# One turn of six raw weight tiles in the MLPs of a two-layer decoder, in place of two rings of three

## The chip, the cores and the metric

The kernel runs on one core of a Trainium2 chip. The metric is the device time of one execution in microseconds (us), the median of several runs. The engines are PE (TensorE: matmuls and transposes; PEld is its loading of weights), DVE (VectorE), ACT (ScalarE), POOL (GpSimd) and SP (SyncE, which here only issues DMAs). Each engine works through its own instructions in order, and an instruction that waits for a semaphore holds up those behind it on its engine.

## The reference

The input is 256 tokens of width D = 2048 in float32, and there are two layers.

```python
h = rmsnorm(x, g);   x = x + dsa_attention(h) @ a_w_out        # layer 1: an indexer picks keys
h = rmsnorm(x, g);   x = x + relu(h @ w_up[0])**2 @ w_down[0]   # D_FF = 8192
k, v = rmsnorm(x, g_kv) @ w_kv                                  # shared keys and values
h = rmsnorm(x, g);   x = x + dilated_attention(h @ b_w_q, k, v) @ b_w_out   # layer 2
h = rmsnorm(x, g);   x = x + relu(h @ w_up[1])**2 @ w_down[1]
out = rmsnorm(x, final_norm)
```

All weights are float32 and are read from memory once.

## The kernel before

**Products.** PE multiplies rounded float32 values ("fp32r"). To keep the accuracy, every operand is split in a high part, a cast (ACT, L190), and a low part, the difference to the original (DVE, L191). A product is then three matmuls, high by high, low by high and high by low (`mm3`, L194 to L196; the same three in `gemm`, L382). A weight tile therefore costs one DMA of 1 MB into a raw tile of 128 x 2 x 1024 values, a cast and a split for each 1024 columns, and then matmuls. The raw tile is free again when its last split has read it. High parts have four buffers, low parts three; within the MLPs one and two more.

**Raw tiles.** Those of the plain products and of all ordinary matrices (attention, projections, down matrix) are `wraw`, a ring of three in the pool `wp`. The pool "mlp", which is open from the middle of each output projection to the end of the MLP, has a second ring of three, `wx`, handed out by `pair_raw` (L239). Its users are the pairs of up tiles, the activations in `add_forms` (`gx`, L302), and in the end the vectors of the final norm (`fg`, L889).

**MLP.** It runs over eight blocks e of 1024 hidden columns: `up(0)`, `up(1)`, `down(0)`, `up(2)`, `down(1)` and so on. `up(e)` computes its 256 x 1024 block by a scheme with seven products for each pair of row blocks (`seven`, for three pairs; each reads two raw tiles, called x0 y0, x1 y1, x2 y2 here, 1 MB each, and forms five or so differences and sums of weights in place on DVE, L724 to L731, before it splits them) and four plain products from two further raw tiles (p0, p1). That is 25 products, 174 matmuls, 25 splits, 12 of those differences, and eight sums on the way out (L740 to L758). `down(e)` is an ordinary product, eight raw tiles d0 to d7, 192 matmuls. Its results are added to the residual `h` by DMAs of POOL that accumulate (L642); only the last block adds on DVE. The squared ReLU and the transposes of an up block are spread between the matmuls of the next block.

**Start of an MLP.** `project` multiplies the attention's output in two halves of 1024 columns. The first part of the depth (`CUT_A` = 8 tiles of 16 in layer 1, `CUT_B` = 14 in layer 2) is done for both halves, then the rest for the first half (O0), then `add_forms` for the first half, the rest for the second half (O1), and `add_forms` for the second half. `add_forms` squares h for the norm (ACT, L324), transposes h (PE, L292), scales it (ACT, L300 and L306), forms four sums on DVE and splits all of it into operands of the up blocks. U0 is `up(0)`.

**Order.** The kernel is written in the Tile language. Its scheduler sorts the instructions of each engine by priority, as they become ready in its own model of time, and buffers that come free in another order lead it to another sequence. All loads of weights go through SP's queue in that sequence, and a load waits at the head of the queue until its raw tile is free.

Of the kernel before, what the change touches and what calls it, by code (L numbers as in the profile page):

```python
# [11 lines left out]
F32 = mybir.dt.float32  # L12
# [5 lines left out]
P = 128  # L18
SEQ = 256
NT = SEQ // P  # L20
D = 2048
KC = D // P
# [19 lines left out]
GW = 1024  # L42
# [9 lines left out]
X0 = 2  # L52
ARRIVE = 2

HI_BUFS, LO_BUFS = 4, 3
HI_MORE, LO_MORE, RAW_MORE = 1, 2, 3

Q_W = NH * HD
# [5 lines left out]
NSM = ID + IH  # L64
# [28 lines left out]
def yoco_kernel(ctx: ExitStack, tc: tile.TileContext, x, a_w_in, a_w_out, w_kv, b_w_q, b_w_out, w_up, w_down,  # L93
# [7 lines left out]
    wp = ctx.enter_context(tc.tile_pool(name="wp", bufs=3))  # L101
# [3 lines left out]
    pools = {}  # L105
# [20 lines left out]
    def b2(dt=F32):  # L126
        return wk.tile([P, 512], dt, name="b2" + ("r" if dt == F32R else ""), tag="b2", bufs=8)
# [7 lines left out]
    def side():  # L135
        return ps2.tile([P, HALF], F32, name="side")
# [51 lines left out]
    def split(hi, lo, src):  # L188

        nc.scalar.copy(hi, src)  # L190
        nc.vector.tensor_tensor(lo, src, hi.bitcast(F32), op=ALU.subtract)  # L191
# [6 lines left out]
    def mm_wide(acc, w_hi, w_lo, xk, first, last):  # L198

        def both():  # L200
            nc.tensor.matmul(acc, w_hi, xk.rearrange("p a t -> p (a t)"), start=first, stop=last)

        if not last:
            both()
        nc.tensor.matmul(acc[:, :SEQ], w_lo, xk[:, 0], start=False, stop=False)
        if last:
            both()
# [28 lines left out]
        lo = lo_of.tile([P, GW], F32R, name="wlo", bufs=LO_BUFS if lo_of is wp else LO_MORE)  # L236
        return hi, lo

    def pair_raw():  # L239
        return pools["mlp"].tile([P, 2, GW], F32, name="wx", bufs=RAW_MORE)  # L240

    def norm_transpose(c4, which):

# [40 lines left out]
    def add_forms(halves, half, which):  # L284
        n, plain, f = halves[half]

        def transposed(c, c2):
            pt = side().rearrange("p (c t) -> p c t", c=2)
            for j in range(2):
                cc = 2 * c2 + j  # L290
                for t in range(NT):
                    nc.tensor.transpose(pt[:, j, t * P:(t + 1) * P], h[t][c][:, cc * P:(cc + 1) * P], ident)  # L292
                g = which * KC + 4 * c + cc
                yield cc, pt[:, j, :], gT[:, g:g + 1]

        if plain is not None:
            for c in range(2):
                for cc, pt, g in transposed(2 * half + c, 1):
                    hi, lo = plain[:, 2 * c + cc - 2, 0, :], plain[:, 2 * c + cc - 2, 1, :]
                    nc.scalar.activation(hi, pt, AF.Copy, scale=g)  # L300
                    nc.vector.scalar_tensor_tensor(lo, pt, g, hi.bitcast(F32), op0=ALU.mult, op1=ALU.subtract)
        gx = pair_raw()[:, :, :n * SEQ].rearrange("p c (j t) -> p c j t", t=SEQ)  # L302
        for c in range(2):
            for c2 in range(n // 2):
                for cc, pt, g in transposed(2 * half + c, c2):
                    nc.scalar.activation(gx[:, c, cc], pt, AF.Copy, scale=g)  # L306
        a11, a21, a12, a22 = gx[:, 0, :, :P], gx[:, 0, :, P:], gx[:, 1, :, :P], gx[:, 1, :, P:]
        s1, s2, s3, s4 = (b2()[:, :n * P].rearrange("p (q t) -> p q t", t=P) for _ in range(4))
        nc.vector.tensor_tensor(s1, a21, a22, op=ALU.add)
        nc.vector.tensor_tensor(s2, a11, s1, op=ALU.subtract)  # L310
        nc.vector.tensor_tensor(s3, a11, a21, op=ALU.subtract)
        nc.vector.tensor_tensor(s4, a12, s2, op=ALU.add)
        for name, v in (("a11", a11), ("a12", a12), ("s4", s4), ("s1", s1), ("s3", s3), ("s2", s2), ("a22", a22)):
            split(f[name][:, :, 0], f[name][:, :, 1], v)
# [37 lines left out]
    def load_w(w, r0, nk, cols, width):  # L352

        n = len(cols) * width
        raw = wp.tile([P, 2, GW], F32, name="wraw", bufs=3).rearrange("p a b -> p (a b)")[:, :nk * n]
        raw = raw.rearrange("p (k c) -> p k c", k=nk)
        joined = all(c == cols[0] + i * width for i, c in enumerate(cols))
        for i, c in enumerate(cols[:1] if joined else cols):
            m = n if joined else width
            nc.sync.dma_start(raw[:, :, i * width:i * width + m],  # L360
                              w[r0:r0 + nk * P, c:c + m].rearrange("(k p) c -> p k c", p=P))
        return raw
# [69 lines left out]
    take_x(0, raw_x, 0, X0)  # L432
    stat = stat_of(xa)
    cols_qi = (COL_QI, COL_QI + HALF)
    raw_w = wp.tile([P, 2, GW], F32, name="wraw", bufs=3)
    for c in range(2):
        nc.sync.dma_start(raw_w[:, 0, c * HALF:(c + 1) * HALF], a_w_in[0, :P, cols_qi[c]:cols_qi[c] + HALF])
    take_x(0, raw_x, X0, 4)
# [21 lines left out]

    def index_keys():

        raw = wp.tile([P, 2, GW], F32, name="wraw", bufs=3).rearrange("p a b -> p (a b)")[:, :KC * NSM]
        nc.sync.dma_start(raw.rearrange("p (k n) -> p k n", n=NSM),
                          a_w_in[0, :, COL_KI:COL_KI + NSM].rearrange("(k p) c -> p k c", p=P))
        acc = ps.tile([P, HALF], F32, name="acc")[:NSM]
        per = KC // 2
        for k0 in range(0, KC, per):
            hi, lo = (b[:, :per * NSM] for b in hi_lo())
            split(hi, lo, raw[:, k0 * NSM:(k0 + per) * NSM])  # L470
            for k in range(k0, k0 + per):
                xk = xa[k // 4][:, k % 4]
                r = slice((k - k0) * NSM, (k - k0 + 1) * NSM)
                mm_wide(acc, hi[:, r], lo[:, r], xk, k == 0, k == KC - 1)
        both = sum_halves(acc)
        pt = side()
        for t in range(NT):
            nc.tensor.transpose(pt[:, t * P:t * P + NSM], both[:, t * P:(t + 1) * P], ident[:NSM, :NSM])
        rstd = st.inv()
        rk = wk.tile([P, NT], F32, name="rk", tag="rk", bufs=2)  # L480
        nc.vector.tensor_scalar(rk, rstd, -SCALE, None, op0=ALU.mult)
        rA.extend((rstd, rk))
        kps = side()
        for t in range(NT):
            r = rstd[:, t:t + 1]
            kk = wk.tile([P, P + 176], F32, name="kk", bufs=1)[:, :P]
            src = pt[:, t * P:t * P + NSM]
            nc.scalar.activation(kk[:, :ID], src[:, :ID], AF.Copy, scale=r)
            nc.vector.tensor_scalar(wi[t], src[:, ID:], r, r, op0=ALU.mult, op1=ALU.mult)
            nc.vector.tensor_scalar(wi[t], wi[t], WI_SCALE, None, op0=ALU.mult)  # L490
            rope(kk[:, :ID].unsqueeze(1), 1, RI // 2, t, True)
            nc.vector.tensor_copy(kk[:, ID:], kk[:, :ID])
            nc.tensor.transpose(kps[:, t * P:(t + 1) * P], kk, ident)
        split(kiT[:, 0], kiT[:, 1], kps[:, :SEQ])
# [176 lines left out]
    def mlp(i, xm, st_in, gains_next, final=None):  # L671
# [4 lines left out]
        def up(e):  # L676
# [8 lines left out]
            c0 = e * GW  # L685
            cl, cr = slice(0, HALF), slice(HALF, GW)

            def raws(k1, tile_of):
                out = []
                for k in (k1, k1 + 4):  # L690
                    r = tile_of()
                    nc.sync.dma_start(r, w_up[i][k * P:(k + 2) * P, c0:c0 + GW].rearrange("(k p) c -> p k c", p=P))
                    out.append(r)
                return out
# [13 lines left out]
            rows = []  # L708

            def plain_rows():  # L710
                rows[:] = raws(2, lambda: wp.tile([P, 2, GW], F32, name="wraw", bufs=3))

            def plain(r, c):
                f = xm[0][2]
# [3 lines left out]
            def seven(half, pair, within=lambda: None, before_last=lambda: None):  # L718

                f = {name: v[:, pair:pair + 2] for name, v in xm[half][2].items() if name[0] != "p"}  # L720
                rx, ry = raws(8 * half + pair, pair_raw)
                b11, b12, b21, b22 = rx[:, :, cl], rx[:, :, cr], ry[:, :, cl], ry[:, :, cr]
                product(b11, (f["a11"], "q1"))
                nc.vector.tensor_tensor(b11, b12, b11, op=sub)  # L724
                product(b21, (f["a12"], "q2"))
                nc.vector.tensor_tensor(b12, b22, b12, op=sub)  # L726
                product(b22, (f["s4"], "q3"))
                nc.vector.tensor_tensor(b22, b11, b22, op=sub)  # L728
                product(b11, (f["s1"], "q5"))
                within()  # L730
                nc.vector.tensor_tensor(b21, b21, b22, op=add)  # L731
                product(b12, (f["s3"], "q7"))
                product(b22, (f["s2"], "q6"))
                before_last()
                product(b21, (f["a22"], "q4"))
# [150 lines left out]
    def final(ustat, w, row0, r2):  # L886


        both = pair_raw().rearrange("p a c -> p (a c)")  # L889
        fg = [both[:, s * HALF:(s + 1) * HALF] for s in range(4)]  # L890
        for s in range(4):
            nc.scalar.dma_start(fg[s], final_norm[s * HALF:(s + 1) * HALF].partition_broadcast(P))
# [35 lines left out]
        nk = GW // P  # L928
# [7 lines left out]
        for k in range(nk):  # L936
            if k % 2 == 0:
                raw = load_w(w, row0 + k * P, 2, (GW, GW + HALF), HALF)
            if k < 6:
                both = new_xt().rearrange("p c a t -> p (c a t)")  # L940
# [18 lines left out]
        for i in range(2):  # L959
            c = slice(i * HALF // 2, (i + 1) * HALF // 2)  # L960
# [41 lines left out]
```

## Time and profile before

| what | value |
|---|---|
| median of 3 runs | 2279.19 us (2277.17 to 2284.68) |
| the profiled execution, its own time | 2276.99 us |
| its span, first to last instruction | 2275.1 us |
| busy: PE, DVE, ACT | 2192.8, 1696.2, 1288.1 us |
| mean granted clock of PE | 0.984 |
| moved by DMA | 434.42 MB, mean 191 GB/s |

The span is what the rows of the profile add up to; the time of a run is about 2 us longer. "Busy" counts instructions under way. PE's matmuls overlap, so a matmul listed with 0.39 us starts 0.227 us after the one ahead of it. In the rows, `a <- b` after a line names what an engine waited for. The weight tile of an up block is `wx` (pairs) or `wraw` (plain), that of all else `wraw`.

### The profile page before, as it was taken

What the parts mean: (1) busy time and instruction counts of PE and PEld (TensorE: products, weight loads), DVE (VectorE), ACT (ScalarE), POOL (GpSimd) and SP (SyncE); (2) the same over time, 40 slices, a digit from 0 to 9 for tenths busy, and PEclk for the clock granted to TensorE, in tenths of its full rate; (3) what the DMA queues carried; (4) which work ended last, traced back from release to release, by engine and by line L of the source; (5) the groups of instructions that cost most, each with busy time, mean ns of one, the idle gap of its engine ahead of it and who ended that gap; (6) DMA issues with size and microseconds to landing.
All of it is one profiled execution on the core that took longest, in us unless ns stands there. A gap on an engine that the chain in (4) does not pass through costs nothing.

```text
span 2275.1 us, 27759 instructions
## 1 busy us (share of the span) xinstructions
PE 2192.8 (96%) x10310; PEld 1798.1 (79%) x10310; DVE 1696.2 (75%) x2267; ACT 1288.1 (57%) x1736; POOL 99.7 (4%) x118
## 2 busy tenths in 40 slices
PE   9999998999999999999999999998999999999998
PEld 7788866778788787788888888876777787787787
DVE  5877769777877867857577777669867867778675
ACT  6545556556656655556455555466556656565564
POOL 0000000011010010010000000000010010010100
PEclk9999999999999999999999999998999999999999
DMA  8554445667767566575554555554677576676754
GB/s 296 166 179 142 160 167 167 204 186 227 227 201 232 181 207 221 149 234 194 171 162 154 161 158 169 171 179 152 219 199 226 179 209 219 187 220 227 202 185 148
DMA packets 164103, 434.42 MB, mean 191 GB/s; under 512 B 12800, under 2 KB 62080, under 8 KB 163968
## 3 DMA queue, kind: packets, MB, share of 16 engines
q1 hardware_dynamic: 146688, 401.25, 52.7%
q0 software_dynamic: 16128, 29.37, 7.3%
q10 hardware_dynamic: 1152, 2.04, 0.3%
q8 instruction: 81, 1.33, 0.2%
q14 instruction: 54, 0.44, 0.1%
HBM read 401.15 MB, written 2.10 MB: 177 GB/s over the span
## 4 chain that ended last, share of the span: by engine, by line
PE 75%; DVE 13%; DMA 9%; ACT 2%; issue 2%; DVEq 0%; ACTq 0%
PE acc L382 58%; DMA wx<-in_w_up_dram 8%; DVE wlo L191 7%; PE acc L194 2%; PE acc L195 2%; PE side L393 2%; PE acc L196 2%; PE side L195 2%; PE side L196 2%; PE side L194 2%; ACT whi L190 1%; DVE wx L726 1%; DVE wx L728 1%; DVE wx L731 1%; DVE b L758 0%
## 5 line engine op out<-in xcount | busy, mean ns | idle before, releaser
L382 PE MATMUL acc<-whi,xt 128*128 128x512 f32 x4160 | 1106.3, 380 | 0.5 <-ACT whi L190 0.5
L191 DVE TENSOR_TENSOR wlo<-wraw,whi 128x1024 fp32r<-128x1024 f32 (+2 forms) x589 | 678.7, 1161 | 345.1 <-ACT whi L190 226.1
L190 ACT CAST whi<-wraw 128x1024 fp32r<-128x1024 f32 (+2 forms) x589 | 587.5, 1002 | 570.4 <-PE acc L382 403.1
L382 PEld LDWEIGHTS acc<-whi,xt 128*128 128x128 f32 x4160 | 737.8, 188 | 138.1 <-ACT whi L190 1.8
L382 PE MATMUL acc<-wlo,xt 128*128 128x512 f32 (+1 forms) x2080 | 618.7, 378 | 5.7 <-DVE wlo L191 5.7
L190 ACT CAST whi<-wx 128x1024 fp32r<-128x1024 f32 x336 | 341.4, 1049 | 309.0 <-DMA wx<-in_w_up_dram 118.8
L382 PEld LDWEIGHTS acc<-wlo,xt 128*128 128x128 f32 x2080 | 371.5, 188 | 79.7 <-DVE wlo L191 7.5
L191 DVE TENSOR_TENSOR wlo<-wx,whi 128x1024 fp32r<-128x1024 f32 x336 | 398.0, 1219 | 46.2 <-ACT whi L190 46.1
L642 POOL DMA_DIRECT2D h<-b x112 | 99.0, 1234 | 2125.9 <-ACT b L641 2107.8
L194 PE MATMUL side<-whi,xt 128*128 128x512 f32 x320 | 128.4, 410 | 38.7 <-ACT whi L190 37.1
L194 PE MATMUL acc<-whi,xf 128*128 128x512 f32 x288 | 121.6, 423 | 13.7 <-ACT whi L190 13.7
L195 PE MATMUL side<-wlo,xt 128*128 128x512 f32 x320 | 131.5, 411 | 2.6 <-DVE wlo L191 2.6
L195 PE MATMUL acc<-wlo,xt 128*128 128x512 f32 x328 | 129.8, 396 | 1.3 <-DVE wlo L191 1.0
L196 PE MATMUL side<-whi,xt 128*128 128x512 f32 x320 | 130.1, 407 | 0.0
L194 PE MATMUL acc<-whi,xt 128*128 128x512 f32 x328 | 129.0, 397 | 0.7 <-ACT whi L190 0.6
L196 PE MATMUL acc<-whi,xt 128*128 128x512 f32 x328 | 128.6, 392 | 0.0
L195 PE MATMUL acc<-wlo,xf 128*128 128x512 f32 x288 | 117.6, 408 | 1.9 <-DVE wlo L191 1.9
L196 PE MATMUL acc<-whi,xf 128*128 128x512 f32 x288 | 115.9, 402 | 0.0
L194 PEld LDWEIGHTS side<-whi,xt 128*128 128x128 f32 x320 | 61.7, 193 | 61.3 <-ACT whi L190 46.7
L726 DVE TENSOR_TENSOR wx<-wx 128x1024 f32<-128x1024 f32 x48 | 58.8, 1225 | 55.6 <-DMA wx<-in_w_up_dram 55.0
L194 PEld LDWEIGHTS acc<-whi,xf 128*128 128x128 f32 x288 | 57.6, 200 | 37.4 <-ACT whi L190 26.2
L393 PE MATMUL side<-ident,b 128*128 128x128 f32 x512 | 77.0, 273 | 4.8 <-ACT b L766 3.5
(198 smaller groups left out, 1890.6 us busy)
## 6 DMA issues: line engine op xcount, KB each, us to landing
wraw<-in_w_down_dram SPq DMA_DIRECT2D x128, 1024.0 KB, 6.2
wx<-in_w_up_dram SPq DMA_DIRECT2D x96, 1024.0 KB, 6.3
wraw<-in_b_w_q_dram SPq DMA_DIRECT2D x192, 256.0 KB, 3.1
wraw<-in_w_up_dram SPq DMA_DIRECT2D x32, 1024.0 KB, 6.4
wraw<-in_a_w_in_dram SPq DMA_DIRECT2D x31, 1024.0 KB, 5.2
h<-b POOLq DMA_DIRECT2D x112, 256.0 KB, 7.8
wraw<-in_a_w_out_dram SPq DMA_DIRECT2D x16, 1024.0 KB, 5.4
wraw<-in_b_w_out_dram SPq DMA_DIRECT2D x16, 1024.0 KB, 5.5
```

What stands on the lines that cost most here:

```text
L190: nc.scalar.copy(hi, src)
L191: nc.vector.tensor_tensor(lo, src, hi.bitcast(F32), op=ALU.subtract)
L194: nc.tensor.matmul(o, a_hi, b_hi, start=start, stop=False)
L195: nc.tensor.matmul(o, a_hi, b_lo, start=False, stop=False)
L196: nc.tensor.matmul(o, a_lo, b_hi, start=False, stop=stop)
L382: nc.tensor.matmul(acc[t][i][:, :c1 - c0], stat(k, a, t), b[:, c0:c1], start=first and a == 0 and b is hi, stop=last and a == 1)
L393: nc.tensor.transpose(pt[:, j * P:(j + 1) * P], sr, ident)
L642: nc.gpsimd.dma_start(hh, part, accum_op=ALU.add)
L726: nc.vector.tensor_tensor(b12, b22, b12, op=sub)
L728: nc.vector.tensor_tensor(b22, b11, b22, op=sub)
L731: nc.vector.tensor_tensor(b21, b21, b22, op=add)
```

## The change

`raw_tile` takes the place of `pair_raw` and of the other requests for raw tiles. While the pool "mlp" is open, it hands out the three tiles of `wp` and the three of the pool in turn, to whatever asks next: pairs, plain tiles, down tiles, the second half of the output projection, `gx`. Outside it hands out the three of `wp` as before. The vectors of the final norm move to a tile that shares the memory of operands no longer needed (`xf4`). Nothing is computed otherwise, and the same number of bytes is held.

```diff
-    def pair_raw():
-        return pools["mlp"].tile([P, 2, GW], F32, name="wx", bufs=RAW_MORE)
+    raw_turn = [0]
+
+    def raw_tile():
+
+        of = wp
+        if "mlp" in pools:
+            of = wp if raw_turn[0] < RAW_BUFS else pools["mlp"]
+            raw_turn[0] = (raw_turn[0] + 1) % (RAW_BUFS + RAW_MORE)
+        return of.tile([P, 2, GW], F32, name="wraw", bufs=RAW_BUFS if of is wp else RAW_MORE)
...
-        gx = pair_raw()[:, :, :n * SEQ].rearrange("p c (j t) -> p c j t", t=SEQ)
+        gx = raw_tile()[:, :, :n * SEQ].rearrange("p c (j t) -> p c j t", t=SEQ)
...
-        raw = wp.tile([P, 2, GW], F32, name="wraw", bufs=3).rearrange("p a b -> p (a b)")[:, :nk * n]
+        raw = raw_tile().rearrange("p a b -> p (a b)")[:, :nk * n]
...
-            def raws(k1, tile_of):
+            def raws(k1):
                 out = []
                 for k in (k1, k1 + 4):
-                    r = tile_of()
+                    r = raw_tile()
...
-                rows[:] = raws(2, lambda: wp.tile([P, 2, GW], F32, name="wraw", bufs=3))
+                rows[:] = raws(2)
...
-                rx, ry = raws(8 * half + pair, pair_raw)
+                rx, ry = raws(8 * half + pair)
...
-        both = pair_raw().rearrange("p a c -> p (a c)")
+        both = pools["mlp"].tile([P, 3 * GW], F32, name="fg", tag="xf4", bufs=1)
```

Lines behind L247 move down by 7. `RAW_BUFS` and `RAW_MORE` are 3.

The scheduler makes other sequences of it. On SP, in the MLP of layer 1, the loads of up and down tiles (`wx` and `wraw` from `w_up` or `w_down`; p0 and p1 are the `wraw` from `w_up`) stood like this before:

```order
L692 DMA wx<-in_w_up_dram 128x2x1024 x4
L360 DMA wraw<-in_w_down_dram 128x2x1024 x6
L692 DMA wraw<-in_w_up_dram 128x2x1024 x2
L360 DMA wraw<-in_w_down_dram 128x2x1024
L692 DMA wx<-in_w_up_dram 128x2x1024 x2
L360 DMA wraw<-in_w_down_dram 128x2x1024
L692 DMA wx<-in_w_up_dram 128x2x1024 x4
L360 DMA wraw<-in_w_down_dram 128x2x1024 x6
```

and now:

```order
L699 DMA wraw<-in_w_up_dram 128x2x1024 x16
L367 DMA wraw<-in_w_down_dram 128x2x1024 x8
L699 DMA wraw<-in_w_up_dram 128x2x1024 x8
L367 DMA wraw<-in_w_down_dram 128x2x1024 x8
L699 DMA wraw<-in_w_up_dram 128x2x1024 x8
```

In the first sequence the `wx` x4 of a block are x2 and y2 together with x0 and y0 of the next one, and d1 stands ahead of them; now the eight up tiles of a block go first and its eight down tiles after them.

On ACT, where O0 ends and O1 begins in layer 1 (`whi<-wraw` are casts of the projection's weights; L324, L300, L306 and the casts of `xt` and `xf` are `add_forms` of the first half), before:

```order
L324 ACTIVATE b_2663,ss<-h_0_86 128x512
L324 ACTIVATE b_2666,ss<-h_1_87 128x512
L300 ACTIVATE xt<-side,gT 128x256 x2
L190 CAST whi<-wraw 128x1024
L300 ACTIVATE xt<-side,gT 128x256 x2
L190 CAST whi<-wraw 128x1024
L306 ACTIVATE wx<-side,gT 128x256 x3
L190 CAST xt<-wx 128x2x128
L306 ACTIVATE wx<-side,gT 128x256
L190 CAST xt<-wx 128x2x128 x2
L190 CAST xf<-b_2701 128x2x128
L190 CAST whi<-wraw 128x1024
```

and now:

```order
L331 ACTIVATE b_2666,ss<-h_1_87 128x512
L307 ACTIVATE xt<-side,gT 128x256 x3
L313 ACTIVATE wraw<-side,gT 128x256 x3
L190 CAST xt<-wraw 128x2x128
L313 ACTIVATE wraw<-side,gT 128x256
L190 CAST xt<-wraw 128x2x128 x2
L190 CAST xf<-b_2701 128x2x128
L190 CAST xf<-b_2702 128x2x128
L190 CAST xt<-b_2703 128x2x128
L190 CAST xf<-b_2704 128x2x128
L190 CAST whi<-wraw 128x1024 x9
```

The casts of O1's weights, which stood ahead of and among the work of `add_forms`, now all stand behind it. On PE, at the same place (L382 and L389 are the projection's matmuls, L292 and L299 the transposes of `add_forms`), before:

```order
L382 MATMUL acc<-whi,xt 128x512 x4
L292 MATMUL side<-ident,h_0_82 128x128
L382 MATMUL acc<-wlo,xt 128x512 x2
L292 MATMUL side<-ident,h_1_83 128x128
L382 MATMUL acc<-whi,xt 128x512 x3
L292 MATMUL side<-ident,h_0_86 128x128
L382 MATMUL acc<-whi,xt 128x512
L382 MATMUL acc<-wlo,xt 128x512
L292 MATMUL side<-ident,h_1_87 128x128
```

and now the first and the last of them:

```order
L389 MATMUL acc<-whi,xt 128x512 x2
L299 MATMUL side<-ident,h_0_82 128x128
L299 MATMUL side<-ident,h_1_83 128x128
L299 MATMUL side<-ident,h_0_86 128x128
L299 MATMUL side<-ident,h_1_87 128x128
L299 MATMUL side<-ident,h_0_82 128x128
```

The sixteen transposes of the first half, which stood between matmuls of O1, now follow each other without one of those between.

More of the change, by code (lines that the diff above doesn't have):

```diff
@@ L53 @@
 ARRIVE = 2
-HI_BUFS, LO_BUFS = 4, 3
+HI_BUFS, LO_BUFS, RAW_BUFS = 4, 3, 3
 HI_MORE, LO_MORE, RAW_MORE = 1, 2, 3
@@ L434, in yoco_kernel @@
     cols_qi = (COL_QI, COL_QI + HALF)
-    raw_w = wp.tile([P, 2, GW], F32, name="wraw", bufs=3)
+    raw_w = raw_tile()
     for c in range(2):
@@ L461, in index_keys @@
     def index_keys():
-        raw = wp.tile([P, 2, GW], F32, name="wraw", bufs=3).rearrange("p a b -> p (a b)")[:, :KC * NSM]
+        raw = raw_tile().rearrange("p a b -> p (a b)")[:, :KC * NSM]
         nc.sync.dma_start(raw.rearrange("p (k n) -> p k n", n=NSM),
```

## The prediction, on record before the result was known

> **What bounds the kernel now.** I read the page first, then what TensorE waits for, then one of these waits on every engine.
>
> ```profile
> span 2275.1 us, 27759 instructions
> PE 2192.8 (96%) x10310; PEld 1798.1 (79%) x10310; DVE 1696.2 (75%) x2267; ACT 1288.1 (57%) x1736; POOL 99.7 (4%) x118
> PE 75%; DVE 13%; DMA 9%; ACT 2%; issue 2%; DVEq 0%; ACTq 0%
> wx<-in_w_up_dram SPq DMA_DIRECT2D x96, 1024.0 KB, 6.3
> ```
>
> PE bounds the program as a whole: it idles for 2275.1 − 2192.8 = 82 us. That is all that better loads can win, apart from clock. The chain of waits gives DMA 9%, far too much for engines that move 1 MB in 6.3 us while PE needs some 40 us for eight such loads; so a few loads must be asked for late. In the two MLPs, from the second up block to the last, PE waits for:
>
> ```profile
> PE side L194 <- ACT whi L190: 14.1, 7, 2.8
> PE acc L194 <- ACT whi L190: 4.5, 10, 0.7
> PE acc L382 <- DVE wlo L191: 3.2, 3, 1.1
> PE side L194 <- ACT whi L190: 17.7, 7, 3.6
> PE acc L194 <- ACT whi L190: 3.0, 8, 0.4
> PE acc L382 <- DVE wlo L191: 2.2, 2, 1.1
> ```
>
> (The first three rows are layer 1, the others layer 2.) Seven waits each: one per up block e = 1 to 7, for a cast of ACT. One of them, in the timelines of SP, ACT, DVE and PE:
>
> ```profile
> 583.28 0.37 SPq L360 DMA_DIRECT2D wraw<-in_w_down_dram  x1
> 587.83 0.37 SPq L692 DMA_DIRECT2D wx<-in_w_up_dram  x1
> 592.74 3.89 ACT L190 CAST whi<-wx 128x1024 fp32r<-128x1024 f32 x4 [6.24 <-DMA wx<-in_w_up_dram]
> 592.74 1.23 DVE L726 TENSOR_TENSOR wx<-wx 128x1024 f32<-128x1024 f32 x1 [2.54 <-DMA wx<-in_w_up_dram]
> 593.88 3.49 DVE L191 TENSOR_TENSOR wlo<-wx,whi 128x1024 fp32r<-128x1024 f32 x3
> 588.73 0.39 PE L196 MATMUL acc<-whi,xf 128*128 128x512 f32 x1
> 591.45 0.39 PE L196 MATMUL acc<-whi,xt 128*128 128x512 f32 x1
> 593.84 0.49 PE L194 MATMUL side<-whi,xt 128*128 128x512 f32 x1 [2.01 <-ACT whi L190]
> 594.79 0.49 PE L194 MATMUL acc<-whi,xf 128*128 128x512 f32 x1 [0.45 <-ACT whi L190]
> ```
>
> The tile is y2, the second tile of the third pair. SP asks for it at 587.83, since its place in the ring of three is free no sooner and a down tile stands ahead of it in SP's queue; it lands 4.9 us later, ACT has been idle 6.24 us, DVE 2.54, PE 2.01 and 0.45. Two sizes for later come from the same rows: 12 matmuls from 588.73 to 591.45 are 0.227 us each at full clock, and three splits of DVE in 3.49 us, one alone listed at about 1.22, follow each other by 1.135.
>
> The wait has a second price, in the column PEclk (the granted clock; start to end, length, then PE, PEld, DVE, ACT, POOL, clock, DMA):
>
> ```profile
> 475.60:519.60 44.00, 40.70 (x176) 32.32 (x175) 38.36 (x37) 27.71 (x31) 3.53 (x4) 1.00 0.63 194
> 565.10:609.30 44.20, 41.74 (x175) 33.68 (x175) 38.83 (x37) 27.83 (x31) 3.53 (x4) 0.96 0.65 196
> 596.20:599.60 3.40, 3.40 (x10) 2.63 (x9) 3.40 (x5) 3.01 (x4) 0.00 (x0) 0.51 0.02 5
> sum 263.30, PE 248.28 PEld 199.45 DVE 230.18 ACT 166.03 POOL 21.18; mean PE 41.38 PEld 33.24 DVE 38.36 ACT 27.67 POOL 3.53
> sum 270.80, PE 251.99 PEld 200.62 DVE 230.55 ACT 166.95 POOL 21.21; mean PE 42.00 PEld 33.44 DVE 38.43 ACT 27.82 POOL 3.53
> 376.00:428.80 52.80, 44.99 (x188) 34.14 (x187) 49.21 (x49) 32.22 (x38) 0.00 (x0) 0.97 0.48 159
> 1577.60:1630.50 52.90, 46.81 (x188) 36.51 (x187) 49.22 (x49) 32.45 (x38) 0.00 (x0) 0.90 0.48 157
> 609.30:654.80 45.50, 45.50 (x210) 37.65 (x209) 30.52 (x30) 25.71 (x34) 3.53 (x4) 1.00 0.73 226
> ```
>
> After the wait of 593.84, in the block of the second row, PE runs 3.4 us at 0.51 of its clock, which loses 1.7 us of work; the first row is a block where it does not. The two sums are the six up blocks e = 2 to 7 of layer 1 and of layer 2, whole: 534.1 us, 44.5 each. Eight of these twelve read 0.96 like the second row, one 0.93, three 1.00; with the blocks e = 1, the two rows behind the sums, that makes some twelve such windows, 20 us. The last row is a down block.
>
> On the clock the Trainium skill ("TensorE: Matmul & The Clock Gate", section "HAM oscillation — how this bites in real kernels") has the rule that PE should have no idle gaps of more than about 3.4 us; a shorter one would by that rule not throttle. This trace disagrees: 2.01 and 0.45 us of idleness came just ahead of a window at 0.51. By the page the waits would cost only their idle time, and the gain would be some 20 us less; by the trace it is whole.
>
> **The change part by part.**
>
> *Steady state.* In the order of SP the change turns a mixed sequence into eight up loads, then eight down loads. With six tiles in turn, y2 takes the place of y0 of its own block, whose last reader is some ten products (of six matmuls, 1.36 us each) before the product that needs y2, and no down load stands ahead of it. The 6.3 us of a load fit. x1 and y1 take the places of the last two tiles of the down block ahead. So the wait at y2 should go in all fourteen up blocks, its clock window with it. What is late next is DVE, the engine behind PE. An up block asks 25 splits and 12 differences of it, 37 × 1.135 = 42.0 us, and 8 half-size sums (4.8 us by an estimate of 0.6 from their 0.68 listed): 46.8 us, against 174 × 0.227 = 39.5 us of PE. Five lo tiles let it run 5 × 1.135 = 5.7 us ahead out of the down block, where it is busy only 30.5 of 45.5 us, and the last sums (1.8 us) fall into the next block: 46.8 − 5.7 − 1.8 = 39.3 us. It just fits. I take 40.5 us for an up block, PE's 39.5 and one for small waits; bounds are 39.5 and 42.0. Twelve blocks: 534.1 − 12 × 40.5 = 48 us won (30 to 60).
>
> Block e = 1 has no down block ahead, and DVE is busy 49.2 of 52.8 us there (45.7 in steps of 1.135 for the listed 1.22); it can come to 48.9, 2 × 3.9 = 8 us won (0 to 12). The starts of the down blocks already show waits for a DVE split (3.2 and 2.2 us in the rows above). With DVE tighter each of the 14 should wait about a split's half more, 0.6: 8 us lost (0 to 16). **Steady sum: −48 − 8 + 8 = −48 us.**
>
> *Start of each MLP, A.* This is where the changed order costs. add_forms for the first half of the columns now stands on ACT ahead of the output projection's remaining casts, on PE its 16 transposes in one piece ahead of the remaining matmuls; before they were mixed. In layer 2 ACT's part of that work runs
>
> ```profile
> 1510.71 0.63 ACT L324 ACTIVATE b<-h 128x512 f32<-128x512 f32 x1 [1.89 <-DVE h L645]
> 1521.33 0.41 ACT L190 CAST xf<-b 128x256 fp32r<-128x256 f32 x1
> L306 ACT ACTIVATE wx<-side,gT 128x256 f32<-128x256 f32 x6 | 2.8, 473 | 1.2 <-PE side L292 1.1
> L300 ACT ACTIVATE xt<-side,gT 128x256 fp32r<-128x256 f32 x4 | 1.9, 468 | 0.7 <-PE side L292 0.7
> 1509.38 0.62 PE L382 MATMUL acc<-wlo,xt 128*128 128x512 f32 x2
> 293.80:318.50 24.70, 24.70 (x117) 19.83 (x117) 16.96 (x28) 14.45 (x30) 0.00 (x0) 1.00 0.57 190
> ```
>
> from 1510.71 to 1521.74, 11.0 us, of which it waited 1.9 for transposes that come sooner when nothing stands between them: 9.1 to 11.0. The projection's half ahead of it ends at 1509.6. So the next cast would be there at 1.1 + 9.1 + 1.05 = 11.3 us after that end (13.2 at most), and all PE has meanwhile are 16 transposes: by the last row 24.7 us less 96 × 0.227 for the projection's matmuls leaves 2.9 us, of which I count 2.2. PE idles 9.1 us (7 to 11) and starts again at half clock, 1.7 us (to 3.4) more. The last row shows that today there is no such gap: 24.70 us of 24.70 busy. A costs 10.8 us per layer, **+21.5 us for two** (17 to 29).
>
> *Start, B and C.* For the second half of the columns the casts of U0's plain products stood ahead of ACT's chain and gave PE 24 matmuls, 5.4 us, to do; now they stand in and behind it. Today U0 shows
>
> ```profile
> PE side L194 <- ACT whi L190: 3.9, 3, 2.9
> PE acc L194 <- ACT whi L190: 3.3, 8, 0.6
> PE side L292 <- ACT wx L306: 2.5, 1, 2.5
> PE acc L194 <- ACT whi L190: 3.5, 7, 1.0
> 318.40:376.00 57.60, 49.02 (x194) 34.90 (x193) 52.49 (x58) 36.81 (x52) 0.00 (x0) 0.94 0.47 162
> ```
>
> (two rows for each layer; the last one is the block in layer 1). Losing all cover would cost 5.4 us per layer, none 0. But DVE is busy 52.5 of 57.6 us in this block, so much of what PE loses here it would have lost later in the block; against that y2 of U0 comes late, since its place waits behind U1's first loads in SP's order, with about 4 us of idle DVE. I take +3.5 in layer 1 and +1 in layer 2, **+4.5 us** (0 to 11).
>
> The vectors of the final norm move to a tile of their own, and `root` with them, out of the last up block: its 3.6 us wait is inside the 534.1 already. The order of both attentions and of the other projections hardly changes; those work from the same three tiles. That costs nothing.
>
> **Sum.** −48 + 21.5 + 4.5 = −22 us against the profiled execution: span 2253, its time 2276.99 − 22 = 2255. The median shown, 2279.19, lies 2.2 us above the profiled time, so I say 2257.
>
> **The rivals.** (1) *The start eats the gain.* A at its upper end (29) and B, C at theirs (11) against a steady gain of 45: within 5 us of before, 2275 to 2280. For it: the first half of U0 is bound by ACT and DVE as well, so delays there are not caught up. Against it: 40 us would need both halves of a layer's start wholly bare. (2) *DVE takes PE's place in the up block: slower.* If the lo splits cannot run ahead, since the down block's own splits hold the five lo tiles up to its end, an up block takes 42.0 us plus the sums that fall in it, about 43; twelve blocks win 534 − 516 = 18, e = 1 nothing, the down starts still lose 8, and the start costs 26 to 30: +16 to +20, 2295 to 2299. It decides from 42.3 us an up block on, where twelve blocks win no more than the 26 us of the start. For it: DVE is busy 38.4 us of an up block today while idling for y2. Against it: in the first row of the clock fence a block of 44.0 us holds 37 DVE operations and some 3.2 us of PE idleness, so without the wait it is already near 41. (3) *The start hurts less.* If PE finds the projection's casts earlier, for instance because the squares wait for no DVE sum, A is half: −33 us, 2246. (4) *The loads don't come sooner*, because SP stands in order and now waits for the oldest of six: each up load behind a down tile not yet freed. Then nothing is won and A, B, C remain: 2305. Against it: y2's place is freed in its own block, and SP has no down load between. (5) *The clock windows stay*, because something other than the wait calls for them: the 20 us are not won, 2277. Against it: they follow the waits in nine of twelve blocks and stand nowhere else in them. The rule of the page named above would have it so.
>
> **How the numbers follow.** Forecast as above 0.48; (3) 0.17; (1) 0.14; (2) 0.13; (4) 0.04; (5) 0.04. About 0.3%, 7 us, is what a measurement of this kernel can tell from no change. Faster by more: 0.48 × 0.96 + 0.17, and a little of (1), 0.66. Within it: the rest of (1) and (5), with a rim of the forecast, 0.17; slower: (2) and (4), 0.17. The likeliest one's own range is 2245 to 2270; with (3) and (1) and the bounds of the steady sum, 2236 to 2284.
>
> **What would show it.** Right: the row "PE side L194 <- ACT whi" falls from 37 us to under 12, up blocks e ≥ 2 take 40 to 41 us with clock 1.00, and two new gaps of 7 to 11 us for `whi` stand between the halves of each output projection. Wrong: up blocks of 42 us or more with waits for `wlo` (rival 2); no long gap ahead of U0 (rival 3); or `wx`'s successor `wraw` still landing within a microsecond of its cast at y2 (rival 4).

## The result, and the profile after

The change takes 2240.26 us (2239.12 to 2240.57, 4 runs) against 2278.48 before (4 runs, one more than in the table above): a ratio of 0.9826, 95% interval 0.9808 to 0.9845. It is 38 us faster where 22 were forecast. The span of the profiled execution falls from 2275.1 to 2238.6, by 36.5 us.

The page of the changed kernel, its span, its busy times, the chain that ended last by engine, and two groups (line, engine, operation, tiles, count; busy, mean ns; idle time ahead of it and its releaser):

```profile
span 2238.6 us, 27840 instructions
PE 2176.6 (97%) x10310; PEld 1792.3 (80%) x10310; DVE 1692.6 (76%) x2267; ACT 1294.3 (58%) x1736; POOL 99.5 (4%) x118
PE 90%; DVE 6%; ACT 2%; issue 1%; DMA 0%; DVEq 0%; ACTq 0%
L194 PE MATMUL side<-whi,xt 128*128 128x512 f32 x320 | 124.9, 400 | 15.2 <-ACT whi L190 14.4
L389 PE MATMUL acc<-whi,xt 128*128 128x512 f32 x4160 | 1109.2, 380 | 7.7 <-ACT whi L190 7.7
```

DMA has left the chain. The wait of 37.1 us at L194 is 14.4; a new one of 7.7 stands at L389, the projection's matmuls. What PE waits for from U1's start to D6, the first four rows in layer 1, the others in layer 2 (us, times, longest):

```profile
PE side L400 <- ACT b L773: 3.2, 2, 1.9
PE acc L194 <- ACT whi L190: 2.5, 5, 0.8
PE side L400 <- DVE xt L403: 0.9, 1, 0.9
PE acc L195 <- DVE wlo L191: 0.3, 2, 0.2
PE side L400 <- ACT b L773: 1.6, 2, 1.4
PE acc L195 <- DVE wlo L191: 0.8, 2, 0.7
PE side L194 <- DVE xt L403: 0.8, 1, 0.8
PE acc L194 <- ACT whi L190: 0.3, 1, 0.3
```

The seven waits for a cast are gone in both layers, and the waits of the down blocks for a split (3.2 and 2.2 us) too.

The example of before has to be read once more. SP's load at 587.83 is not y2: nothing in the block waits for it, and it lands 7.6 us later, at 595.39. The load that DVE and ACT wait for is the one ahead of it, asked for at 585.55, 0.02 us after the last split of the tile whose place it takes. So the four `wx` loads in a row are y2 with x0, y0 and x1 of the next block, the two in a row are y1 and x2, and the down load at 583.28 did not hold y2 up in SP's queue. From the list of who waits for the load at 585.55, its time to landing, and what DVE waited for in layer 1 before:

```profile
  DVE wx L726: 2.5, 1
DMA to landing us min/median/max: 7.1/7.1/7.1
DVE wx L726 <- DMA wx<-in_w_up_dram: 25.0, 13, 3.0
```

The thirteen waits of the last row are seven for y2 and six for y1, the second tile of the second pair; y1 was late in these blocks too, but PE did not wait there in the example. After the change DVE waits for no load in these blocks. In the block of the example SP now asks for y2 at 582.91, some 17 us ahead of DVE's first work on it (the split at 599.98); before it was 7.2. The up blocks (first row one of them; the sums the six e = 2 to 7 of layer 1 and of layer 2; the last sum the two blocks e = 1):

```profile
582.91 0.37 SPq L699 DMA_DIRECT2D wraw<-in_w_up_dram  x1
575.20:615.00 39.80, 39.80 (x176) 32.58 (x175) 38.28 (x37) 27.04 (x30) 3.52 (x4) 1.00 0.70 209
sum 238.90, PE 238.73 PEld 195.33 DVE 229.48 ACT 168.63 POOL 21.13; mean PE 39.79 PEld 32.55 DVE 38.25 ACT 28.10 POOL 3.52
sum 238.60, PE 238.44 PEld 195.08 DVE 229.17 ACT 168.40 POOL 21.17; mean PE 39.74 PEld 32.51 DVE 38.20 ACT 28.07 POOL 3.53
sum 98.00, PE 88.95 PEld 67.78 DVE 96.98 ACT 64.95 POOL 0.00; mean PE 44.48 PEld 33.89 DVE 48.49 ACT 32.48 POOL 0.00
```

534.1 us became 477.5, PE busy in all of them at clock 1.00; an up block between its first and last matmul takes 39.5 us. The two blocks e = 1 went from 105.7 to 98.0.

What the start of an MLP costs, from the end of O0 to the first matmul of U1: the first two rows before (layer 1, layer 2), the others after.

```profile
293.80:376.10 82.30, 73.72 (x309) 54.77 (x309) 69.46 (x85) 51.17 (x81) 0.00 (x0) 0.96 0.50 170
1509.40:1577.70 68.30, 58.73 (x237) 42.62 (x236) 63.15 (x80) 45.11 (x75) 0.00 (x0) 0.93 0.49 166
```

```profile
293.60:394.10 100.50, 80.23 (x308) 59.41 (x307) 73.22 (x88) 56.11 (x85) 0.00 (x0) 0.85 0.41 142
1496.40:1579.40 83.00, 62.51 (x236) 44.96 (x235) 67.09 (x83) 49.76 (x79) 0.00 (x0) 0.84 0.45 159
```

It is 18.2 us longer in layer 1 and 14.7 in layer 2: 33 us given back. In layer 1 PE idles 20.3 us there instead of 8.6, and it is busy for 6.5 us longer, since the mean clock falls to 0.85. The first gap in the timelines of ACT and PE in layer 1, and the stretch around it, at half clock:

```profile
293.80 0.63 ACT L331 ACTIVATE b<-h 128x512 f32<-128x512 f32 x1 [11.64 <-DVE h L652]
304.40 0.41 ACT L190 CAST xf<-b 128x256 fp32r<-128x256 f32 x1
304.72 3.88 ACT L190 CAST whi<-wraw 128x1024 fp32r<-128x1024 f32 x4
294.47 0.38 PE L299 MATMUL side<-ident,h 128*128 128x128 f32 x2
301.27 0.69 PE L299 MATMUL side<-ident,h 128*128 128x128 f32 x2 [0.56 <-ACT wraw L313]
305.81 1.22 PE L389 MATMUL acc<-whi,xt 128*128 128x512 f32 x2 [3.85 <-ACT whi L190]
297.80:311.40 13.60, 8.41 (x22) 5.37 (x23) 10.27 (x18) 9.44 (x17) 0.00 (x0) 0.50 0.00 0
```

O0 ends at about 294.5 and O1 begins at 305.81; in between PE has sixteen transposes, with waits between them. ACT itself idled 11.64 us ahead of the first square, since the casts of O1 stand behind the squares in its order; in own_start_u0 below it makes two of them there, at 292.21 and 294.93. O1's loads were not late: the last one landed at 289.04, 15.7 us ahead of ACT's first cast of them at 304.72.

So the balance is: up blocks −56.6, blocks e = 1 −7.7, down blocks −5.2 (the twelve between up blocks, 552.2 before and 547.0 now), start of the MLPs +33, the rest of the program +0.3, together −36.2 of the 36.5.

### The profile page after: what moved, and what is told of

The parts are those of the page before. It is cut to its first block, busy times and chain, and to the rows that moved or that the text cites. A ratio compares the mean times of both kernels' runs of the same rounds, so it can differ in the third digit from the quotient of the medians.

```text
span 2238.6 us, 27840 instructions
## 1 busy us (share of the span) xinstructions
PE 2176.6 (97%) x10310; PEld 1792.3 (80%) x10310; DVE 1692.6 (76%) x2267; ACT 1294.3 (58%) x1736; POOL 99.5 (4%) x118
## 4 chain that ended last, share of the span: by engine, by line
PE 90%; DVE 6%; ACT 2%; issue 1%; DMA 0%; DVEq 0%; ACTq 0%
PE acc L389 59%; PE acc L195 6%; PE acc L196 5%; PE acc L194 5%; PE side L195 4%; PE side L194 4%; PE side L196 4%; DVE wlo L191 2%; PE side L400 2%; ACT whi L190 1%; DVE wraw L733 1%; DVE wraw L735 0%; DMA wraw<-in_w_up_dram 0%; ACT b L331 0%; DVE wraw L731 0%
## 5 line engine op out<-in xcount | busy, mean ns | idle before, releaser
L190 ACT CAST whi<-wraw 128x1024 fp32r<-128x1024 f32 (+2 forms) x925 | 928.0, 1020 | 786.9 <-PE acc L389 510.1
L191 DVE TENSOR_TENSOR wlo<-wraw,whi 128x1024 fp32r<-128x1024 f32 (+2 forms) x925 | 1072.9, 1181 | 370.1 <-ACT whi L190 251.0
L389 PE MATMUL acc<-whi,xt 128*128 128x512 f32 x4160 | 1109.2, 380 | 7.7 <-ACT whi L190 7.7
L389 PEld LDWEIGHTS acc<-whi,xt 128*128 128x128 f32 x4160 | 739.7, 189 | 147.5 <-ACT whi L190 10.1
L389 PE MATMUL acc<-wlo,xt 128*128 128x512 f32 (+1 forms) x2080 | 619.2, 379 | 0.4 <-DVE wlo L191 0.4
L389 PEld LDWEIGHTS acc<-wlo,xt 128*128 128x128 f32 x2080 | 372.8, 188 | 75.4 <-DVE wlo L191 2.3
L194 PE MATMUL side<-whi,xt 128*128 128x512 f32 x320 | 124.9, 400 | 15.2 <-ACT whi L190 14.4
L194 PE MATMUL acc<-whi,xt 128*128 128x512 f32 x328 | 129.3, 399 | 4.9 <-ACT whi L190 4.9
L196 PE MATMUL side<-whi,xt 128*128 128x512 f32 x320 | 127.1, 397 | 0.0
L194 PE MATMUL acc<-whi,xf 128*128 128x512 f32 x288 | 114.9, 400 | 3.8 <-ACT whi L190 3.5
L196 PE MATMUL acc<-whi,xf 128*128 128x512 f32 x288 | 112.9, 392 | 0.0
L194 PEld LDWEIGHTS side<-whi,xt 128*128 128x128 f32 x320 | 61.1, 192 | 30.7 <-ACT whi L190 16.9
L194 PEld LDWEIGHTS acc<-whi,xt 128*128 128x128 f32 x328 | 62.1, 190 | 22.1 <-ACT whi L190 9.8
L400 PEld LDWEIGHTS side<-ident,b 128*128 128x128 f32 x512 | 62.1, 140 | 21.4 <-ACT b L773 6.2
L195 PEld LDWEIGHTS side<-wlo,xt 128*128 128x128 f32 x320 | 61.6, 192 | 16.2 <-DVE wlo L191 2.0
L648 ACT ACTIVATE b<-acc,ri 128x512 f32<-128x512 f32 x112 | 71.0, 686 | 4.1
```

Of the source, the lines that this page charges most:

```text
L194: nc.tensor.matmul(o, a_hi, b_hi, start=start, stop=False)
L195: nc.tensor.matmul(o, a_hi, b_lo, start=False, stop=False)
L196: nc.tensor.matmul(o, a_lo, b_hi, start=False, stop=stop)
L389: nc.tensor.matmul(acc[t][i][:, :c1 - c0], stat(k, a, t), b[:, c0:c1], start=first and a == 0 and b is hi, stop=last and a == 1)
L400: nc.tensor.transpose(pt[:, j * P:(j + 1) * P], sr, ident)
L648: nc.scalar.activation(part, acc, AF.Copy, scale=scale()[:, t:t + 1])
```

## The experiments

All ratios are against the kernel before, measured beside it. The theory after the result was: (a) the steady gain of 70 us (56.6, 7.7 and 5.2) is that of the turn of six, and is bounded by PE; (b) the loss of 33 us is not needed for it: it comes from the order in which ACT does `add_forms` and the casts of O1.

**Turn only in the MLP's own loads.** A flag `turning` keeps the old tiles for the projection's second half and `gx` (`pair` is set for `gx` and the pairs of up tiles). This is own_start; in own_start_u0 the last line added is `turning[0] = e > 0`:

```diff
-        if "mlp" in pools:
+        if "mlp" in pools and not turning[0]:
+            of = pools["mlp"] if pair else wp
+        elif "mlp" in pools:
             of = wp if raw_turn[0] < RAW_BUFS else pools["mlp"]
...
         open_scope("mlp")
+        turning[0] = False
...
         for e in range(NE):
+            turning[0] = True
             up(e)
```

> The turn of six begins only with the first up block; the second half of the output projection and `gx` keep the tiles that they had before, and with them ACT has its old order there. My theory: the fourteen later up blocks keep their whole gain (about 70 us against before), and the 33 us lost around the two output projections and U0 come back, since they came from the projection's loads and `gx` standing in the turn: 2240 - 33 = 2207, 2203 to 2216. Rival: the loss comes from U0's own loads standing in the turn (its y2 behind U1's first tiles): then no more than a few us come back, 2232 to 2243.

> As own_start, but U0 too keeps its old tiles (pairs in one ring of three, plain products in the other); the turn begins with U1. My theory: U0 is held by DVE and ACT either way, so the time equals own_start's within 4 us, 2203 to 2212. Rival (U0's loads in the turn cost the start): 2207 here while own_start stays at 2232 to 2243.

Measured: own_start 2217.25 us (2216.57 to 2219.36), ratio 0.9732 (0.9718 to 0.9747); own_start_u0 2208.80 us (2207.93 to 2209.64), ratio 0.9693 (0.9679 to 0.9708). The second beats the change by 31 us. The two starts of own_start_u0:

```profile
293.80:376.10 82.30, 73.66 (x309) 54.62 (x308) 69.43 (x85) 51.20 (x81) 0.00 (x0) 0.96 0.50 170
1478.80:1547.10 68.30, 59.31 (x237) 42.95 (x237) 63.24 (x80) 45.05 (x75) 0.00 (x0) 0.93 0.48 165
```

The starts are those of before to 0.1 us, and its twelve later up blocks take 39.5 us each as in the change: gain and loss are separate. The expectations held in part: of the 33 us, 23 came back with the projection and `gx` out of the turn, and U0's own loads were worth another 8.4, which I had put at under 4; own_start lies 1 us above its range. In own_start U0 of layer 2 waits first for a split that stands on DVE behind the sums and splits of `add_forms`, then for a cast behind a late load:

```profile
1506.63 0.54 PE L195 MATMUL acc<-wlo,xt 128*128 128x512 f32 x1 [4.19 <-DVE wlo L191]
1510.80 1.23 DVE L736 TENSOR_TENSOR wraw<-wraw 128x1024 f32<-128x1024 f32 x1 [2.97 <-DMA wraw<-in_w_up_dram]
1511.83 0.79 PE L194 MATMUL side<-whi,xt 128*128 128x512 f32 x1 [2.95 <-ACT whi L190]
```

The load is that of the second tile of U0's first pair. SP asked for it at 1505.54, 0.1 us after DVE's last split of `gx` there; own_start_u0 has no wait for a load at this place. Block by block, own_start is 2.0 us faster than own_start_u0 in U0 of layer 1 and slower in D0 of layer 1 (2.9), U0 of layer 2 (4.9) and the last down block (3.1): U0's loads in the turn do not cost in principle, but in layer 2 the places and the order that they get do.

**The reverse.** The projection, `gx` and U0 in the turn, from U1 on two rings of three (`turning[0] = True` at the scope's start, then `e == 0`).

> The reverse: the turn of six for the projection's second half, `gx` and U0, and from U1 on the two old rings of three. My theory: the loss without the gain, 2278 + 33 = 2311, 2303 to 2318, with up blocks of 43 to 46 us and half-clock windows in most of them. Rival (the gain comes from somewhere else, for instance from the larger lead that the first loads take): 2278 to 2290, with up blocks under 42 us.

Measured: 2310.34 us (2308.86 to 2311.51), ratio 1.0139 (1.0124 to 1.0154), 32 us slower than before. From U1 to U7 of layer 1 PE again waits like this, and two up blocks there:

```profile
PE side L194 <- ACT whi L190: 14.6, 7, 2.5
494.20:538.00 43.80, 41.62 (x175) 33.48 (x175) 38.41 (x37) 27.63 (x31) 3.52 (x4) 0.96 0.64 195
583.40:627.20 43.80, 40.74 (x176) 32.51 (x176) 38.48 (x37) 27.84 (x32) 3.52 (x4) 1.00 0.64 198
```

The loss without the gain, as expected: seven waits, 43.8 us, a clock of 0.96 in seven of the twelve up blocks e = 2 to 7. Since this kernel holds the norm's vectors in their own tile, as the change does, that edit is not where the gain comes from.

**Five in turn.** own_start with `RAW_MORE = 2`.

> As own_start with five tiles in turn instead of six. If the turn as such is what helps (any tile for any load), five serve as well: 2207 to 2215. My theory is that the places decide: y2 then takes p0's place, still free some six products ahead, but the first down tile takes the place of p1, whose last product ends the up block, so that each down block starts with most of a load's 6 us as a wait: 14 times 4 to 6 us, 2207 + 56 to 84 = 2263 to 2291, unless the scheduler takes another order.

Measured: 2249.98 us (2245.91 to 2250.38), ratio 0.9868 (0.9852 to 0.9885): 33 us slower than own_start with six, which is neither of the two expectations. PE's waits from U1 to U7 of layer 1, what DVE waited for in the up blocks of layer 1 and of layer 2, and an up block of each layer:

```profile
PE acc L195 <- DVE wlo L191: 3.2, 11, 0.4
DVE wraw L736 <- DMA wraw<-in_w_up_dram: 7.0, 6, 1.3
DVE wraw L736 <- DMA wraw<-in_w_up_dram: 14.9, 6, 2.8
476.60:517.60 41.00, 40.36 (x176) 32.43 (x175) 38.31 (x37) 26.94 (x31) 3.52 (x4) 1.00 0.66 205
1667.10:1709.60 42.50, 40.94 (x175) 32.25 (x175) 38.29 (x37) 27.69 (x31) 3.55 (x4) 1.00 0.64 195
```

The twelve up blocks together are 25 us longer than in own_start (8.6 in layer 1, 16.8 in layer 2), with many small waits of PE for splits. The down blocks do not start with a wait for a load, and y2 comes early enough. What comes late is y1, which with five tiles takes the place of x0: in the block e = 3 of layer 1 SP asks for it at 567.26, and DVE waits for it until 574.20. DVE waits so once in each of the twelve blocks, 21.9 us in all, and in none of own_start. So the places decide, as I had expected, but another tile's than the one that I had looked at. Of the rest of the 33 us, 11 lie between O0 and D0 of the two MLPs, and the end of the program is 3 us shorter than in own_start. Why p1's place did not hold up the down blocks I did not follow further.

**How much room DVE has.** In own_start_u0, four (in dve_plus8 eight, 2, 5, 8 and so on to 23) of the 25 splits of each up block are done twice:

```diff
                 split(hi, lo, src)
+                again[0] += 1
+                if again[0] % 25 in (4, 10, 16, 22):
+                    nc.vector.tensor_tensor(lo, src, hi.bitcast(F32), op=ALU.subtract)
```

> own_start_u0 with four of the 25 splits of each up block computed twice on DVE (the same values again, so nothing else changes): 4.5 us more DVE work in a block. The prediction's sum for DVE (46.8 us of work less 5.7 ahead less 1.8 behind = 39.3 against PE's 39.5) leaves no room: U0 and U1, where DVE is the bound, get 4.5 us longer each (18 us in all), and the twelve later ones 2.5 to 4.5 each: 2209 + 48 to 72 = 2257 to 2281, with waits for `wlo` in them. Rival: that blocks stand at 39.52 us shows a DVE with room, which it finds in the down blocks: only the 18 us of U0 and U1, 2222 to 2232.

> The same with eight splits twice, 9.1 us more in a block. If DVE is bound already, each further split costs its 1.135 us in full: dve_plus4 plus 16 blocks times 4.5 = 73 us, 2325 to 2355. If there was room of a few us, the twelve blocks begin to lengthen only here: 2209 + 36 + up to 12 times 4 = 2245 to 2293.

Measured: 2260.41 us (2260.07 to 2260.76), ratio 0.9920 (0.9904 to 0.9937), and 2342.52 (2341.78 to 2343.26), ratio 1.0280 (1.0265 to 1.0295). An up block and the down block behind it, in own_start_u0, with four and with eight more:

```profile
557.20:642.40 85.20, 85.20 (x384) 70.15 (x383) 69.17 (x66) 53.63 (x64) 7.04 (x8) 1.00 0.72 222
```

```profile
567.90:656.30 88.40, 86.08 (x384) 69.90 (x383) 73.74 (x70) 53.73 (x64) 7.04 (x8) 1.00 0.69 214
PE acc L194 <- ACT whi L190: 11.6, 13, 1.6
```

```profile
582.00:675.50 93.50, 89.05 (x383) 70.46 (x382) 77.85 (x74) 54.11 (x63) 7.04 (x8) 0.98 0.66 203
```

4.5 us more of DVE cost 3.2, the next 4.5 cost 5.1, more than their own time; the clock is 0.98 there. Both times lie in the ranges that I had given for a DVE that is bound. So DVE had between one and two us of room in a block of 39.5, though it is busy only 69 of 85 us in the pair of blocks. It is the next bound of the up block. I had expected the waits to carry the name `wlo`; nearly all of them carry `whi`, because half of the casts are of differences that DVE has to form first (second row of the second fence: U2 to U7 of layer 1).

**The start, part by part.** `gx` alone out of the turn (gx_own), and the projection alone out of it (proj_own); U0 stands in the turn in both. Of the edits below the first is gx_own's, where `gx=True` gives a tile of the pool's three, which the turn uses too (not of a ring of its own, as the expectation has it), the second proj_own's:

```diff
-        gx = raw_tile()[:, :, :n * SEQ].rearrange("p c (j t) -> p c j t", t=SEQ)
+        gx = raw_tile(gx=True)[:, :, :n * SEQ].rearrange("p c (j t) -> p c j t", t=SEQ)
...
+            turning[0] = False
             gemm(stat, range(cut, KC), w, 0, (n * GW, n * GW + HALF), residual(st, n))
+            turning[0] = True
```

> As the change, but `gx` keeps a ring of its own in the pool; the projection's second half and all of U0 stand in the turn. On ACT `add_forms` then still stands ahead of all of O1's casts. My theory: that order, and not a late load, makes the gap of PE: the time stays near the change's, 2234 to 2244, and PE idles some 7 us between the two halves of each projection. Rival: the gap comes from `gx` waiting for a tile that a weight holds; without that it shrinks, 2217 to 2226.

> The counterpart: the projection's second half keeps the three old tiles, `gx` and the up tiles stand in the turn. ACT again has `add_forms` ahead of O1's casts. My theory (the order on ACT): 2234 to 2244. Rival (the projection's loads in the turn are what comes late): 2217 to 2226.

Measured, two runs each: gx_own 2228.45 us (ratio 0.9779, 0.9760 to 0.9799), proj_own 2219.42 (0.9740, 0.9720 to 0.9759). gx_own lies between its two ranges. proj_own misses my theory's and lies in its rival's, but not by the rival's way, as layer 1 shows. The starts of gx_own, then those of proj_own:

```profile
294.40:390.70 96.30, 77.93 (x308) 57.28 (x307) 73.30 (x88) 54.16 (x83) 0.00 (x0) 0.88 0.39 134
1492.80:1568.40 75.60, 61.08 (x236) 43.14 (x235) 66.52 (x83) 48.89 (x78) 0.00 (x0) 0.89 0.42 144
```

```profile
293.90:389.60 95.70, 77.99 (x308) 57.22 (x307) 73.03 (x88) 54.06 (x84) 0.00 (x0) 0.88 0.40 135
1492.10:1558.10 66.00, 57.47 (x236) 42.59 (x235) 62.69 (x80) 45.19 (x75) 0.00 (x0) 0.92 0.49 170
1493.40 0.63 ACT L333 ACTIVATE b<-h 128x512 f32<-128x512 f32 x1 [1.89 <-DVE h L654]
1494.03 1.03 ACT L190 CAST whi<-wraw 128x1024 fp32r<-128x1024 f32 x1
```

Three of these four starts have the late casts of O1 on ACT, and in each of the three O1 ends 11.3 to 11.4 us later after O0 than before, with the same gap of PE ahead of it (3.85 us in its last part, as in the change). In the fourth, layer 2 of proj_own, a cast stands between the squares (last row), O1 is on time, and the start is 2.3 us shorter than before. So proj_own's time comes from two unlike layers: layer 1 loses 13.4 us, layer 2 gains 2.3. That fits the order on ACT as the cause, and so do all 20 starts of the ten kernels: in seven ACT casts none of O1's weights from the end of O0 until at least 9.5 us later, and O1 begins 10.6 to 11.2 us after that end; in the thirteen others O1 begins at once. No run changed that order alone. I had looked at the order of layer 1 alone when I set the expectation for both layers. In gx_own, moreover, the second half's gap is gone: there U0's plain products are again between the transposes. Neither the projection's loads nor `gx` is the single cause; either one in the turn can lead the scheduler to that order.

## Why the prediction was right or wrong

Direction and mechanism were right, and the time lies inside the range, near its lower end; the sizes were off in both directions. By its steps, against the spans:

- **The wait at y2 goes, its clock window with it.** Right: no such wait in either layer, clock 1.00 in the twelve blocks. turn_start_only brings both back. The reading behind it was partly wrong: y2 was asked for at 585.55 and not at 587.83, took 7.1 us and not 4.9, and waited for its place, not for a down load ahead of it in the queue. What the change needed, a place that is free earlier, was right. The rows quoted there hold fourteen windows (24 us) and not some twelve; the two at the start of U1 in layer 2 stay (0.93).
- **40.5 us for an up block.** Mis-sized: 39.5, its lower bound; 56.6 us won instead of 48. DVE's sum of 39.3 against PE's 39.5 came close: it leaves 0.2 us of room, and dve_plus4 shows one to two. The one us "for small waits" was added without a row for it, and there are none.
- **U1 at 48.9 us.** Right: 49.0, bound by DVE (96.98 of 98.0 us busy in the two blocks); 7.7 us won of 8 forecast.
- **Down blocks lose 8 us to DVE.** Wrong in sign: they win 5.2. The waits for a split at their start, 5.4 us, are gone. DVE had idled for loads itself, 2.54 us for y2 in the row quoted there and 25.0 us in layer 1 in all, so it gets time back when these waits end, which fits; I counted only what PE would ask of it.
- **A, 10.8 us per layer.** Nearly right: O1 ends 12.2 us (layer 1) and 11.6 us (layer 2) later after O0's end than before, and O1 begins 11.2 us after O0's end where 11.3 were worked out, by the path worked out, ACT's chain with a cast behind it. Of the idleness, 6.8 us in layer 1 where 9.1 were forecast, only 3.85 carry the name `whi`; the rest lies between the transposes. So the signs given for it, waits of 7 to 11 us for `whi` and a row at L194 of under 12 (it is 14.4), did not hold.
- **B and C, 4.5 us.** Mis-sized: 33.0 − 23.8 = 9.2, close to the upper end of 11. The assumption that U0, bound by DVE, would have lost this time later anyway does not hold. And the clock was cut for longer than the one window I counted: for 13.6 us around the first gap of layer 1, and 0.85 over that whole start against 0.96. How the 9.2 us divide between these two I did not separate.
- **Rivals.** DVE as the next bound (2) is real, but one step further on: it decides if DVE gets 1.5 us more work, not now. Rivals (4) and (5) are refuted by the rows above. (3) did not occur. The start hurt more, 33 us, on the way to (1)'s 40, and the larger steady gain paid for it. That the total comes out within 17 us of the forecast is in part luck, since the two misses have opposite signs.

The sum was therefore short by 21 us of gain (69.5 instead of 48) and by 7 us of loss (33 instead of 26).

## What to carry to other kernels

Where the same load is waited for at the same place of every iteration, though the transfers as a whole have time to spare, look when that load was asked for, and whose place it waits for. Match the request to the load that ends the wait by its landing: here the next request in the queue was taken for it. All tiles of one size in one turn, in the order of their use, gave y2 a place that is free earlier, and it was asked for 17 us ahead of its use in place of 7. Such a change reaches everything that shares the tiles, so give it only to the loop that needs it: the same turn was worth 70 us in the loop and cost 33 at its entrance, and the version that has it only from the second iteration on keeps the gain without the loss. After a wait is gone, sum the work of the engine behind it against the new block, its own idle time for the same load included.

## What was not expected of the hardware

The clock fell after far shorter idle times than one window. Cutting the traces of this case's ten kernels in stretches of 3.413 us, with the phase at which the granted clock changes, and adding PE's gaps over 0.1 us in each: of 67 stretches at full clock with 1.8 us or more of idleness, 65 were followed by a stretch at half clock; of some 320 with 0.3 to 1.3 us none was; in between 22 of 63. Two examples from before, each a stretch and the one behind it (1.68 us idle, then full clock; 2.62 idle, then half):

```profile
500.70:504.10 3.40, 1.72 (x8) 1.10 (x6) 0.97 (x2) 0.57 (x1) 0.00 (x0) 1.00 0.95 318
504.10:507.50 3.40, 2.43 (x9) 1.66 (x10) 3.40 (x4) 3.40 (x5) 0.00 (x0) 1.00 0.29 118
1978.60:1982.00 3.40, 0.78 (x2) 0.37 (x2) 2.32 (x3) 2.31 (x3) 0.00 (x0) 1.00 0.68 281
1982.00:1985.40 3.40, 3.40 (x9) 2.63 (x9) 3.40 (x5) 2.34 (x3) 0.00 (x0) 0.51 0.00 0
```

So in these traces what counts is the share of a stretch, about half of it, and a gap of 2 us may or may not be caught, by how it lies to the stretches' edges. That fits the twelve up blocks of before: in the three whose wait cost no clock the idlest stretch holds 1.3 to 1.7 us of idleness, in the nine others 1.5 to 2.6. This is read from traces, no run varied a gap on purpose. The Trainium skill ("TensorE: Matmul & The Clock Gate", section "Part 1: The HAM clock gate (the "warmup" mystery)") states the window of 3413 ns and that it runs free of the kernel, and these traces agree with both: within a run the clock changes on one grid of 3.413 us, but for its last change, and that grid lies otherwise to the start of the span in each of the ten runs. The Trainium skill's bound of a whole idle window, in the same section, does not agree.
